# RWKV-7 and pooling layer on one core: the per-pair bonus goes through DRAM, nine gate projections before the dense stage instead of four, and a new order of the work

## The chip, the cores and the metric

The kernel runs on one core of a Trainium2 chip. The metric is the device time of one execution in microseconds (us). The kernel before takes 1591.02 us, the median of three runs (1590.69 to 1591.06).

## The reference

The function computes one inference step of two layers on T = 576 tokens, 512 of a prompt and 8 x 8 of sampled sequences. Each layer is a residual branch behind an RMS norm. The first is RWKV-7 time mixing, in short:

```python
r, k, v, z = xr @ w_r, xk @ w_k, xv @ w_v, xg @ w_z           # 1024 -> 2048 each
decay = exp(-exp(-softplus(-(w0 + tanh(xw @ w1) @ w2)) - 0.5))
a = sigmoid(a0 + (xa @ a1) @ a2)
# per head of 64, over the tokens in turn:
Sa = S @ a_t                                                  # a_t is -kk, b_t is kk * a
S = S * w_t + Sa[:, None] * b_t + v_t[:, None] * k_t ;  y_t = S @ r_t
y = group_norm(y) * gn_g + gn_b
bonus = sum(r * k * r_k, per head) * v
out = ((y + bonus) * silu(z)) @ w_o                           # 2048 -> 1024
```

The second layer is a causal pooling mixer: u, z = x @ w_in, averages of u over windows of 2, 4, 8 and 16 tokens, a grouped product, a SiLU gate and an output product. A last norm and the new states are the other outputs.

## The kernel before, in words

The 2048 inner channels are 16 "pairs" of heads, 128 channels each, on the 128 partitions; KC is 16. A projection of one pair is 8 slices of the input (KD) times two halves of 288 tokens (HT) times three matmuls (high by high, high by low, low by high part of fp32): 48 matmuls. Casts on ScalarE make the high part of the weights (wh), subtractions on VectorE or GpSimd the low part (wl).

The work comes in four stretches.

- **The front**, a loop over the pairs: the k and r projections (L493), low-rank products for decay and a (L576), the scan L of log decays (L622), and from its exponentials Pc, Pp and Pi the scaled operands: RAt (L643 from r, L670 from the normed k), BK (L679), its scaled copy BS and the transposes BT (L694), and rk (L658). RAt, BK, BT and rk are spilled to DRAM by SP.
- **The recurrence**, a loop over the pairs with the tokens in chunks of 64. `vproj(m)` projects v for a pair (L875, `oov`), stores vs and its transpose, loads rk and makes the bonus: a product over the head (L902, `oob`), a product with vs in place (L906) and the addition of gn_b (L910). `prep(m)` makes the chunk matrices (L941, `paA`) and inverts them: a loop on GpSimd (L1012, L1018) on X, X to the DRAM tile xd (L1025), the blocks TI back (L1032), transposes T of them on VectorE (L1039), small products `paz` and `pax`. `recur(m)` runs the chain of eight steps, one per chunk: PE state product L1124, ScalarE rhs L1137, PE TI product L1141, ScalarE UV L1146, PE product with BKT L1157, VectorE state update L1169. The outputs `yy` (L1240, L1245) go beside it. `after(m)` normalises y; its last step is L1336 (`pay`) and L1341, which adds vs, the bonus, and the result is written to yb_d (L1346).
- **The gates**. `zgate(m)` projects z for m below NZ = 4 (L1362, `ooz`), takes the SiLU (L1367) and writes z_d (L1371). The other twelve are projected in the dense stage (`gz`, L343 to L345) with their SiLU at L1438.
- **The dense stage**: yb and, for m below NZ, z are read back, GpSimd multiplies them (L1439), the product is cast (GH); then w_o (`go`), the pooling layer and the norms.

Everything up to the gates is registered as an operation of a plan; `Plan.order` emits them by a heap on a number, WHEN of the operation's label plus STEP times the pair, out of the table OFFS. An operation is emitted only when what it needs has been emitted and a buffer of each kind in its list `use` is free. So the table sets the order of the instructions on every engine, SP's DMA queue among them. The dense stage is ordered by the tile scheduler. There, z uses the five buffers with the tag "t" (`ctmp`, L1401), yb three, and the products of `proj` six PSUM banks, two to a gate.

Of the kernel before, what the change touches and what calls it, by code (L numbers as in the profile page):

```python
# [46 lines left out]
def constants():  # L47
# [26 lines left out]
    for rho in range(3):  # L74
# [9 lines left out]
F_STEP, R_STEP, Z_STEP = 18.2314, 26.0177, 19.4548  # L84
# [17 lines left out]
    ),  # L102
# [7 lines left out]
    ),  # L110
# [7 lines left out]
    ),  # L118
# [15 lines left out]
    ),  # L134
    "x": (
        "44.02 336.91 19.73 "
# [1469 lines left out]
```

## Time and profile before

| what | us |
|---|---|
| median of three runs | 1591.02 |
| lowest and highest | 1590.69, 1591.06 |
| the profiled execution, its own time | 1591.95 |
| its span, first to last instruction | 1590.1 |
| TensorE busy | 1404.9 (88%) |
| VectorE busy | 899.1 (57%) |
| ScalarE busy | 672.5 (42%) |
| GpSimd busy | 623.3 (39%) |

The span is what lies between the first and the last instruction in the trace. A busy share is an average over the whole span, in which the stretches differ: the front lies at about 0 to 404 us, the recurrence at about 479 to 1002, the gates at 1002 to 1101, and the rest of the dense stage ends at 1590. In a row of a timeline the first number is the start, the second the duration in us, then engine, line, operation, the tile written and the tiles read, and how many instructions were merged; in brackets stands the idle time of the engine just before, and what ended it.

### The profile page before, as it was taken

Reading aid. Unit: us, or ns where it says so; the run is one execution under the profiler, and the core shown is the slowest. Engines: PE = TensorE matmul, PEld = TensorE weight load, DVE = VectorE, ACT = ScalarE, POOL = GpSimd, SP = SyncE. Lnnn points to the kernel's source line nnn. Section 1 sums busy time; section 2 is a strip of 40 time slices with the busy share of each in tenths; the row PEclk is TensorE's granted clock in tenths of the full one; section 3 lists DMA queues with packets and bytes.
Section 4 is the critical chain, followed back from the end, with each engine's and each line's share of the span. In section 5 each row is a group of like instructions: output and inputs, shape, how many; then the busy total and the mean of one; then the engine's idle time right before and its main releaser. Section 6 shows DMA issues by size and latency. Waiting matters only on the chain.

```text
span 1590.1 us, 31516 instructions
## 1 busy us (share of the span) xinstructions
PE 1404.9 (88%) x12032; PEld 1276.7 (80%) x12032; DVE 899.1 (57%) x1840; ACT 672.5 (42%) x1683; POOL 623.3 (39%) x1297
## 2 busy tenths in 40 slices
PE   3678989998458888998889888999999999999996
PEld 2568989998447776776677756899999999999995
DVE  5877777677464655666566654353335474555223
ACT  3453655655114555555555553243223423334221
POOL 1025666665217656665666650042001141443000
PEclk8668999999678999999999986999999999999998
DMA  3025655556657667766777664463223232222221
GB/s 131 17 109 188 223 195 186 176 176 233 209 126 166 150 158 167 163 160 164 166 159 172 147 167 135 137 229 101 80 80 94 88 102 84 90 88 96 80 68 72
DMA packets 236751, 219.86 MB, mean 138 GB/s; under 512 B 149772, under 2 KB 184312, under 8 KB 236472
## 3 DMA queue, kind: packets, MB, share of 16 engines
q1 hardware_dynamic: 236600, 217.84, 48.3%
q8 instruction: 95, 1.56, 0.4%
q14 instruction: 56, 0.46, 0.1%
HBM read 151.76 MB, written 66.02 MB: 137 GB/s over the span
## 4 chain that ended last, share of the span: by engine, by line
PE 62%; DVE 16%; ACT 10%; issue 4%; POOL 3%; DMA 3%; SPq 1%; ACTq 0%; DVEq 0%; POOLq 0%
PE oov L875 4%; PE ch L1157 3%; PE ch L1141 3%; PE paA L941 3%; PE ch L1124 3%; DVE RAt L670 3%; PE zz L345 2%; PE u L345 2%; PE go L345 2%; PE go L343 2%; PE oo L345 2%; PE oo L343 2%; PE u L344 2%; PE u L343 2%; PE zz L344 2%
## 5 line engine op out<-in xcount | busy, mean ns | idle before, releaser
L1012 POOL TENSOR_TENSOR tm<-X,R 108x84 f32<-108x84 f32 (+23 forms) x465 | 148.7, 320 | 176.2 <-DMA xd<-X 77.8
L1018 POOL TENSOR_TENSOR X<-X,tm 108x84 f32<-108x84 f32 (+23 forms) x465 | 155.3, 334 | 36.4
L875 PE MATMUL oov<-X,wh_o 128*128 128x288 f32 x512 | 123.7, 330 | 18.9 <-ACT wh_o L773 18.9
L1169 DVE SCALAR_TENSOR_TENSOR SV<-SV,pcs,ch 64x64 f32<-64x64 f32 x192 | 53.8, 280 | 131.5 <-PE ch L1157 128.9
L329 ACT CAST wh_z<-wf_z 128x1024 fp32r<-128x1024 f32 x42 | 44.2, 1052 | 182.9 <-PE go L344 63.6
L493 PE MATMUL kvk<-X,wh_z 128*128 128x288 f32 x480 | 103.4, 309 | 2.1 <-DVE X L475 2.1
L330 DVE TENSOR_TENSOR wl_z<-wf_z,wh_z 128x1024 fp32r<-128x1024 f32 x42 | 60.3, 1435 | 72.7 <-ACT wh_z L329 72.7
L875 PEld LDWEIGHTS oov<-X,wh_o 128*128 128x128 f32 x512 | 83.3, 199 | 21.5 <-ACT wh_o L773 19.3
L1141 PE MATMUL ch<-rhs,TI 128*128 128x128 f32 x256 | 64.7, 336 | 27.6 <-ACT rhs L1137 23.4
L329 ACT CAST wh_o<-wf_o 128x1024 fp32r<-128x1024 f32 x42 | 44.2, 1053 | 103.2 <-issue 30.8
L1157 PEld LDWEIGHTS ch<-UV,BKT 128*128 128x128 f32 x256 | 40.0, 195 | 58.3 <-ACT UV L1146 45.6
L493 PEld LDWEIGHTS kvk<-X,wh_z 128*128 128x128 f32 x480 | 82.5, 202 | 2.3 <-DVE X L475 2.3
L1157 PE MATMUL ch<-UV,BKT 128*128 128x128 f32 x256 | 62.8, 328 | 23.2 <-ACT UV L1146 19.4
L493 PE MATMUL kvr<-X3h,wh_o 128*128 128x256 f32 (+1 forms) x256 | 80.8, 315 | 0.6 <-ACT wh_o L773 0.6
L493 PE MATMUL kvr<-X3h,wl_o 128*128 128x256 f32 (+1 forms) x256 | 78.5, 306 | 2.9 <-DVE wl_o L777 2.5
L1439 POOL TENSOR_TENSOR yb<-yb,z 128x576 f32<-128x576 f32 x16 | 29.7, 1867 | 130.6 <-DMA z<-z_d 95.2
L493 PE MATMUL kvr<-X3l,wh_o 128*128 128x256 f32 (+1 forms) x256 | 78.1, 305 | 0.0
L875 PE MATMUL oov<-X,wl_o 128*128 128x288 f32 x256 | 77.8, 304 | 0.2 <-DVE wl_o L777 0.2
L1141 PEld LDWEIGHTS ch<-rhs,TI 128*128 128x128 f32 x256 | 39.7, 195 | 44.9 <-ACT rhs L1137 40.8
L493 PE MATMUL kvk<-X,wl_z 128*128 128x288 f32 x240 | 73.7, 307 | 0.0
L1146 ACT COPY UV<-ch 64x64 f32<-64x64 f32 x256 | 53.2, 208 | 47.3 <-PE ch L1141 45.1
L941 PE MATMUL paA<-RA,BK 64*128 64x128 f32 x576 | 60.1, 312 | 13.4 <-DVE RA L974 3.8
(319 smaller groups left out, 4738.2 us busy)
## 6 DMA issues: line engine op xcount, KB each, us to landing
bk_d<-BK SPq DMA_DIRECT2D x16, 576.0 KB
ra_d<-RAt SPq DMA_DIRECT2D x16, 576.0 KB
bkt_d<-BT SPq DMA_DIRECT2D x64, 144.0 KB
RA<-ra_d SPq DMA_DIRECT2D x32, 288.0 KB
BK<-bk_d SPq DMA_DIRECT2D x16, 576.0 KB
BKT<-bkt_d SPq DMA_DIRECT2D x64, 144.0 KB
wf_o<-in_w_r SPq DMA_DIRECT2D x16, 512.0 KB
wf_o<-in_w_v SPq DMA_DIRECT2D x16, 512.0 KB
```

What stands on the lines that cost most here:

```text
L329: (hi_eng or S).copy(out=hi, in_=src) if (hi_eng or S) is S else hi_eng.tensor_copy(hi, src)
L330: (lo_eng or V).tensor_tensor(out=lo, in0=src, in1=hi.bitcast(F32), op=ALU.subtract)
L343: PE.matmul(out, wh, xh, start=first, stop=False)
L344: PE.matmul(out, wh, xl, start=False, stop=False)
L345: PE.matmul(out, wl, xh, start=False, stop=last)
L493: PE.matmul(o, w_[:, k, :rows], x_[:, c0:c1], start=k == 0 and i == 0, stop=k == KD - 1 and i == 2)
L875: PE.matmul(buf(*pk)[:, :HT], w_[:, k, :], hs(x_, h), start=k == 0 and i == 0, stop=k == KD - 1 and i == 2)
L941: PE.matmul(pts[q][:, c - c0, :], buf("BK", m)[r0:r0 + 64, c, :], ra(m, q, c), start=True, stop=True)
L1012: E.tensor_tensor(out=tm[:, :nq, :nt], in0=X[:, :nq, s:s + 1].broadcast_to([108, nq, nt]), in1=R[:, s:s + 1, s + 1:].broadcast_to([108, nq ...
L1018: E.tensor_tensor(out=X[:, :nq, s + 1:], in0=X[:, :nq, s + 1:], in1=tm[:, :nq, :nt], op=ALU.add)
L1141: PE.matmul(tile()[:, lo + 128:lo + 256], TI[:, c, :], buf(*rk), start=True, stop=True)
L1157: PE.matmul(buf(*ck)[:, 256:384], buf("BKT", m)[:, c], buf("UV", m)[:, :, c, :], start=True, stop=True)
```

## The change

Three things change. The bonus of a pair (vs after L910) is written by SP to a new DRAM tile bv_d, and `after` reads it back into a tile vr of two buffers, which L1341 uses; vs has two buffers instead of four, and the matmuls of the v projection count as users of vs. NZ is 9 instead of 4. And the whole table OFFS and its steps are new (two lines of it stand for all).

```diff
-F_STEP, R_STEP, Z_STEP = 18.2314, 26.0177, 19.4548
+F_STEP, R_STEP, Z_STEP = 17.1191, 29.6201, 28.3583
...
-        "-16.37 603.57 140.77 382.00 360.77 1129.03 152.36 -54.00 92.74 1132.20 291.83 68.40 1063.08 386.45 151.82 "
+        "-151.11 95.56 101.96 -88.30 -67.95 631.36 -20.94 612.15 -192.57 533.35 634.24 563.57 -145.54 31.51 -124.91 "
...
-NTI, NRA, NW3, NVS, NZ = 3, 4, 4, 4, 4
+NTI, NRA, NW3, NVS, NZ = 3, 4, 4, 2, 9
...
+    bv_d = [dp.tile([128, T], F32, name=f"bv_d{i}") for i in range(KC)]
...
-           "vs": ([128, T], NVS), "vt": ([128, 2, 9, 32], 1), "rk": ([128, T], 1), "zs": ([128, T], 1),
+           "vs": ([128, T], NVS), "vr": ([128, T], 2), "vt": ([128, 2, 9, 32], 1), "rk": ([128, T], 1), "zs": ([128, T], 1),
...
-                mms.append(op("PE", 400, f, need=ws[k // 4] + [xve[k]] + mms[-1:], use=[pk, (f"WO{k // 4}", "v", m)], due=due + .1 * (8 * h + k),
+                mms.append(op("PE", 400, f, need=ws[k // 4] + [xve[k]] + mms[-1:], use=[pk, uvs, (f"WO{k // 4}", "v", m)], due=due + .1 * (8 * h + k),
...
+        def f():
+            SP.dma_start(out=bv_d[m], in_=vs())
+        by["bv", m] = op("SP", 1000, f, need=by["bv", m], use=[uvs], due=due + 7)
...
-        ug, uv = ("sq", m, 1), ("vs", m)
-        lv = by["bv", m]
+        ug, uv = ("sq", m, 1), ("vr", m)
+        n0, plan.n = plan.n, 60
+
+        def f():
+            SP.dma_start(out=buf(*uv), in_=bv_d[m])
+        lv = [op("SP", 1000, f, need=[by["bv", m]], use=[uv], due=due)]
+        plan.n = n0
...
-                                       in1=buf("vs", m)[:, 64 * c0:64 * c1], op0=ALU.mult, op1=ALU.add)
+                                       in1=buf("vr", m)[:, 64 * c0:64 * c1], op0=ALU.mult, op1=ALU.add)
```

Line numbers of the changed kernel are one higher than those of the kernel before up to the bonus, five higher from there, ten higher from the group norm on. Three places show the new order.

**TensorE, the boundary of two pairs in the recurrence.** `ch` is the chain's PSUM tile, one number per pair. Before, from the state product of a pair's last step to the next pair's first:

```order
L1124 MATMUL ch_7299<-SV_6987,RA_5952 128x128
L1048 MATMUL paz_7690<-T_7626,AB_6839 32x32 x16
L1141 MATMUL ch_7299<-rhs_7_7685,TI_4144 128x128
L902 MATMUL oob_1_7713<-rk_7253,cst 128x288
L902 MATMUL oob_0_7717<-rk_7253,cst 128x288
L1157 MATMUL ch_7299<-UV_7015,BKT_7175 128x128
L1062 MATMUL pax_7732<-TI_4145,ZM_7707 32x32 x16
L875 MATMUL oov_1_7750<-X_63,wh_o 128x288 x2
L875 MATMUL oov_1_7750<-X_63,wl_o 128x288
L875 MATMUL oov_1_7750<-X_63,wh_o 128x288 x2
L875 MATMUL oov_1_7750<-X_63,wl_o 128x288
L1124 MATMUL ch_7766<-SV_7454,RA_6419 128x128
```

Now, from the state product of the pair's seventh step on:

```order
L1129 MATMUL ch_7262<-SV_7089,RA_6271 128x128
L1129 MATMUL ch_7732<-SV_7559,RA_6741 128x128
L1146 MATMUL ch_7262<-rhs_6_7730,TI_4165 128x128
L876 MATMUL oov_0_7424<-X_63,wh_o 128x288 x2
L876 MATMUL oov_0_7424<-X_63,wl_o 128x288
L1162 MATMUL ch_7262<-UV_7119,BKT_6949 128x128
L903 MATMUL oob_0_7755<-rk_7675,cst 128x288
L1053 MATMUL paz_7757<-T_7726,AB_6907 32x32 x16
L1129 MATMUL ch_7262<-SV_7089,RA_6271 128x128
L903 MATMUL oob_1_7793<-rk_7675,cst 128x288
L1346 MATMUL pay_1_7796<-cst,yc_7403 64x64 x8
L1146 MATMUL ch_7262<-rhs_7_7788,TI_4165 128x128
```

and, fourteen rows further:

```order
L946 MATMUL paA_4_0_7876<-RA_7681,BK_7683 128x128
L946 MATMUL paA_4_1_7877<-RA_7681,BK_7683 128x128
L946 MATMUL paA_4_0_7876<-RA_7681,BK_7683 128x128
L946 MATMUL paA_4_1_7877<-RA_7681,BK_7683 128x128
L1162 MATMUL ch_7262<-UV_7119,BKT_6949 128x128
L1146 MATMUL ch_7732<-rhs_0_7734,TI_4166 128x128
```

The next pair's first state product (L1129 into ch_7732) stands ahead of the seventh step's TI product, the two `oob` stand behind the products with BKT, and the next pair's first TI product (L1146) directly follows the last product with BKT (L1162).

**VectorE, one pair of the front.** Before, from the scan L on:

```order
L622 SCALAR_TENSOR_TENSOR L_2600<-scan,sg 128x592
L694 STREAM_TRANSPOSE BT_2569<-BS_2538 128x9x2x32
L643 TENSOR_TENSOR RAt_2656<-kvr_0_2602,Pc_2648 64x5x64 x2
L670 SCALAR_TENSOR_TENSOR RAt_2656<-ks_2370,dv,Pp_2662 64x9x64 x2
L643 TENSOR_TENSOR RAt_2656<-kvr_1_2514,Pc_2648 64x4x64 x2
L679 TENSOR_TENSOR BK_2685<-kh_2682,Pi_2624 128x9x64
L658 SCALAR_TENSOR_TENSOR rk_2687<-kvr_1_2514,par,kh_2682 128x256
L658 SCALAR_TENSOR_TENSOR rk_2687<-kvr_0_2602,par,kh_2682 128x320
L592 TENSOR_SCALAR rc_2740<-ss_2733 96x12
```

Now:

```order
L623 SCALAR_TENSOR_TENSOR L_2611<-scan,sg 128x592
L671 SCALAR_TENSOR_TENSOR RAt_2616<-ks_2370,dv,Pp_2613 64x9x64 x2
L695 STREAM_TRANSPOSE BT_2622<-BS_2619 128x9x2x32 x2
L644 TENSOR_TENSOR RAt_2616<-kvr_0_2590,Pc_2665 64x5x64 x2
L644 TENSOR_TENSOR RAt_2616<-kvr_1_2562,Pc_2665 64x4x64 x2
L659 SCALAR_TENSOR_TENSOR rk_2718<-kvr_0_2590,par,kh_2691 128x320
L659 SCALAR_TENSOR_TENSOR rk_2718<-kvr_1_2562,par,kh_2691 128x256
L680 TENSOR_TENSOR BK_2722<-kh_2691,Pi_2652 128x9x64
L612 SCALAR_TENSOR_TENSOR kq_2502<-ks_2370,dv,sn_0_2740 128x288
```

The two L670 operations (now L671) have moved from behind the first products of RAt to directly behind the scan.

**ScalarE, the entry of the dense stage.** Before:

```order
L1438 ACTIVATE z_11918<-gz_0_11922 128x288
L329 CAST wh_z<-wf_z 128x1024
L1438 ACTIVATE z_11918<-gz_1_11947 128x288
L329 CAST wh_o<-wf_o 128x1024
L329 CAST GH<-yb_11888 128x576
L1438 ACTIVATE z_11979<-gz_0_11983 128x288
L1438 ACTIVATE z_11979<-gz_1_12008 128x288
L329 CAST GH<-yb_11895 128x576
L1438 ACTIVATE z_12040<-gz_0_12044 128x288
L329 CAST GH<-yb_11902 128x576
```

Now, from the cast of the first dense weights on:

```order
L329 CAST wh_z<-wf_z 128x1024
L1377 ACTIVATE zs_12203<-ooz_1_12205 128x288
L329 CAST wh_z<-wf_z 128x1024
L329 CAST wh_o<-wf_o 128x1024
L329 CAST GH<-yb_12252 128x576
L329 CAST GH<-yb_12259 128x576
L329 CAST GH<-yb_12266 128x576
L329 CAST wh_z<-wf_z 128x1024
L329 CAST GH<-yb_12273 128x576
L329 CAST GH<-yb_12280 128x576
L1448 ACTIVATE z_12317<-gz_0_12321 128x288
```

The first SiLU of a gate projected in the dense stage (L1448 now, L1438 before) stood ahead of the first cast GH; now it stands behind five of them.

Elsewhere: the v projection of a pair still ends two pairs ahead, and its last matmuls stand in pair 13; `oob` has moved from the pair itself to two pairs ahead. On SP, the reads of vr, of a quarter of BKT and of rk now stand between the writes of xd and the reads of TI. From the first matmul of `go` on no engine's order has changed.

## Rows read from the trace of the kernel before

**Rows 1.** Busy time by stretch: one front pair, one recurrence pair, gates, the rest.

```profile
core 0: us, PE busy (x) PEld busy (x) DVE busy (x) ACT busy (x) POOL busy (x), PEclk, DMA share, GB/s
264.93:283.08 18.15, 17.44 (x133) 16.81 (x133) 12.70 (x18) 10.21 (x23) 11.07 (x13) 1.00 0.54 179
...
706.40:738.80 32.40, 29.09 (x347) 23.10 (x346) 20.40 (x61) 17.62 (x63) 20.86 (x66) 1.00 0.70 162
...
1024.80:1101.30 76.50, 76.47 (x576) 76.47 (x577) 31.00 (x27) 28.71 (x49) 27.51 (x15) 1.00 0.59 195
1101.30:1590.10 488.80, 473.96 (x3522) 470.02 (x3520) 221.47 (x324) 142.65 (x184) 90.36 (x105) 0.99 0.26 84
```

**Rows 2.** Chain of waits by line, within one front pair (283.08 to 301.22).

```profile
by line: DVE RAt L670 33.5%; DVE L L622 9.3%; issue 9.0%; PE kvr L493 8.9%; PE sw L576 7.1%; DVE rk L658 5.2%; ACT kh L648 4.8%; DVE RAt L643 4.7%; ACT kq L552 4.3%; ACT ta L580 4.3%; ACT Pi L629 4.3%; DVE BT L694 4.3%; DVE BK L679 4.2%; AC
```

**Rows 3.** Timeline of TensorE, pairs 7 and 8 of the recurrence.

```profile
760.05 0.49 PE L1124 MATMUL ch<-SV,RA 128*128 128x128 f32 x2
...
761.95 0.49 PE L1157 MATMUL ch<-UV,BKT 128*128 128x128 f32 x2 [0.52 <-ACT UV L1146]
...
763.13 0.49 PE L1124 MATMUL ch<-SV,RA 128*128 128x128 f32 x2
...
767.50 0.49 PE L1141 MATMUL ch<-rhs,TI 128*128 128x128 f32 x2
767.83 1.14 PE L902 MATMUL oob<-rk,cst 128*128 128x288 f32 x4
769.11 0.49 PE L1157 MATMUL ch<-UV,BKT 128*128 128x128 f32 x2
...
771.05 0.38 PE L1124 MATMUL ch<-SV,RA 128*128 128x128 f32 x2
771.36 0.49 PE L941 MATMUL paA<-RA,BK 64*128 64x128 f32 x4
...
774.54 0.49 PE L1141 MATMUL ch<-rhs,TI 128*128 128x128 f32 x2
```

**Rows 4.** Timeline of SP and VectorE in pair 8: xd, TI, L1341, transposes.

```profile
783.73 1.45 SPq L1025 DMA_DIRECT2D xd<-X  x3
788.90 1.80 SPq L1032 DMA_DIRECT2D TI<-xd  x4
...
792.91 0.54 DVE L1341 SCALAR_TENSOR_TENSOR sq<-pay,par,vs 128x320 f32<-128x320 f32 x1
...
795.27 0.91 DVE L1039 STREAM_TRANSPOSE T<-TI 64x256 f32<-64x256 f32 x2
```

**Rows 5.** All L670 operations: shortest, median and longest ns, first and last start.

```profile
L670 DVE SCALAR_TENSOR_TENSOR RAt<-ks,dv,Pp x18: 809/819/2631, 264.9 to 406.3; 64x576 f32<-64x576 f32 x18
```

**Rows 6.** Timeline of GpSimd beside the L670 operations of one pair.

```profile
283.13 0.73 POOL L565 TENSOR_TENSOR ll<-lf,lh 96x256 fp32r<-96x256 f32 x1
283.82 1.28 POOL L777 TENSOR_TENSOR wl_o<-wf_o,wh_o 128x512 fp32r<-128x512 f32 x1
```

**Rows 7.** Timeline of TensorE, ScalarE and GpSimd from the gates into the dense stage.

```profile
1009.40 0.40 PE L1362 MATMUL ooz<-X,wl_z 128*128 128x288 f32 x1 [0.26 <-DVE wl_z L777]
...
1024.83 0.40 PE L343 MATMUL gz<-X,wh_z 128*128 128x288 f32 x1 [1.32 <-ACT zs L1367]
...
1031.65 0.41 ACT L1438 ACTIVATE z<-gz 128x288 f32<-128x288 f32 x1 [6.87 <-PE gz L345]
...
1041.41 0.68 ACT L329 CAST GH<-yb 128x576 fp32r<-128x576 f32 x1 [2.63 <-POOL yb L1439]
...
1039.95 4.71 POOL L1439 TENSOR_TENSOR yb<-yb,z 128x576 f32<-128x576 f32 x3 [95.24 <-DMA z<-z_d]
1046.75 5.45 POOL L1439 TENSOR_TENSOR yb<-yb,z 128x576 f32<-128x576 f32 x3 [2.08 <-DMA yb<-yb_d]
```

**Rows 8.** Timeline of SP and VectorE at the first pair's TI.

```profile
469.76 1.80 SPq L1032 DMA_DIRECT2D TI<-xd  x4
...
473.26 0.91 DVE L1039 STREAM_TRANSPOSE T<-TI 64x256 f32<-64x256 f32 x2 [6.37 <-DMA TI<-xd]
```

More of the change, by code (lines that the diff above doesn't have):

```diff
@@ L87 @@
     "s": (
[14 rows of a table removed]
[13 rows of a table added]
     ),
     "g0": (
[6 rows of a table removed]
[6 rows of a table added]
     ),
     "g1": (
[6 rows of a table removed]
[6 rows of a table added]
     ),
     "f": (
[6 rows of a table removed]
[6 rows of a table added]
     ),
     "e": (
[6 rows of a table removed]
[6 rows of a table added]
     ),
     "x": (
-        "44.02 336.91 19.73 "
+        "125.02 116.05 49.68 "
     ),
     "p": (
[8 rows of a table removed]
[8 rows of a table added]
     ),
     "v": (
-        "523.57 1040.30 854.62 1041.49 129.97 1050.03 1050.15 1052.16 1054.58 -11.47 1063.70 1064.27 1066.70 429.73 "
-        "1043.85 1031.21 1049.44 1053.03 1055.05 1059.61 1058.09 1065.52 166.08 1044.70 70.84 74.27 374.57 419.80 "
-        "1042.69 1121.40 429.26 1139.32 1120.68 66.40 1026.65 "
+        "490.19 531.12 527.84 532.83 -112.45 538.37 538.11 543.05 547.18 -47.55 555.18 556.90 560.36 561.56 535.91 "
+        "-89.79 538.53 544.24 546.14 554.86 -36.96 556.90 21.20 556.90 -74.53 -187.33 138.86 -181.42 555.22 561.25 "
+        "-230.65 562.80 562.47 -77.48 565.04 -318.29 "
     ),
     "c": (
[8 rows of a table removed]
[8 rows of a table added]
     ),
     "o": (
-        "-16.37 603.57 140.77 382.00 360.77 1129.03 152.36 -54.00 92.74 1132.20 291.83 68.40 1063.08 386.45 151.82 "
-        "-153.18 1134.73 98.25 89.73 185.29 1110.79 1134.06 994.42 1144.50 1072.56 1155.82 "
[3 rows of a table added]
     ),
     "y": (
-        "1496.73 1503.45 67.64 1505.39 58.47 1505.69 1086.16 1509.62 "
+        "1034.50 1043.91 0.32 1022.28 116.00 1029.10 482.43 1057.96 "
     ),
     "z": (
-        "1450.95 67.43 197.50 90.55 1484.35 1127.54 171.35 975.59 155.00 1473.82 1496.06 409.58 450.91 190.92 1498.08 "
-        "1002.12 1504.12 87.17 133.84 436.59 406.24 1111.84 1108.83 1019.99 "
+        "1018.95 1021.87 1030.19 1037.69 1036.94 1041.83 1042.12 -42.15 1042.68 1047.39 533.11 1048.28 1047.67 "
+        "-218.40 1049.68 1048.36 1048.24 1050.32 -144.58 1051.39 -61.30 1049.12 1060.25 57.96 "
     ),
```

109 rows, old and new, of the table OFFS are left out of this document.

## The prediction, made before the change was run

> **What bounds the kernel now.** I read the busy time by stretch first [rows 1]. From 1101.30 us on TensorE is busy 473.96 of 488.80 us; on every engine the instruction order of that stretch, from the first w_o product on, is unchanged, so I cost it at nothing. In the gate stretch before it (1024.80 to 1101.30) TensorE is busy 76.47 of 76.50 us: this part is bounded by matmuls and nothing else. Ahead of that lie two loops over the 16 pairs. One pair of the front takes 18.15 us [rows 1], with TensorE busy 17.44 of it; its chain of waits gives VectorE's two L670 operations 33.5% [rows 2]. One pair of the recurrence takes 32.40 us. There TensorE is busy 29.09 us, VectorE 20.40, ScalarE 17.62, GpSimd 20.86 and the DMA engines 70% [rows 1]: none is full, so the eight-step chain and what TensorE does in its gaps set the time. A bare step is the distance from one state product L1124 at 760.05 to the next at 763.13 [rows 3], 3.08 us; in it TensorE idles 0.52 us for ScalarE's UV, and from L1157 to the next L1124 it has 1.18 us to fill.
>
> The profiled execution took 1591.95 us, 0.93 above the median of the three runs, 1591.02; 1.85 us of it lie outside the span of 1590.1. The sum is made on 1591.95, and 0.93 comes off at the end. A difference under 0.2%, 3.2 us, is about what a measurement of this kernel cannot tell from no change.
>
> **The spill and the read-back.** Sixteen writes and sixteen reads of 128x576 f32 (0.295 MB each) are added, 0.59 MB a pair. In the recurrence DMA moves 162 GB/s over 32.4 us [rows 1], 5.25 MB a pair, so this is 11% more; 70% busy becomes about 78%. I cost the traffic at nothing: the idle 30% hides it. Without that cover it would be 0.59 MB at 162 GB/s, 3.6 us a pair. No compute instruction is added by it, and the final L1341 only waits for a DMA where it waited for ScalarE. VectorE holds, behind L1341, the state update L1169: a late read would stop the chain; this is a rival below. The read goes out after the xd writes, which end being issued at 785.18 in pair 8, and L1341 comes at 792.91 [rows 4], 7.7 us later.
>
> **Does v run further ahead?** By the order it does not: the v projection stays two pairs ahead, with the same number of matmuls in nearly every gap, and still ends in pair 13; only the bonus product oob moves, from the pair itself to two pairs ahead. So pairs 14 and 15 stay poorly filled, as now; I cost them at 0, with 3 us either way.
>
> **The pair boundary.** Here the new order bites. Now, from the last TI product of a pair (767.50) to the first of the next (774.54) TensorE takes 7.04 us [rows 3] and has hardly a gap in it: two oob, L1157, pax, six oov, L1124, four paA, 32 yy, sixteen paA. In the new order the next pair's L1124 is issued one step earlier, and both oob go between L1157 and the following TI product of the last two steps. The oob take the 1.28 us from 767.83 to 769.11 and L1124 the 0.31 from 771.05 to 771.36 [rows 3]; 7.04 - 1.28 - 0.31 = 5.45 us are left between the two TI products. That saves 1.6 us a pair if the two oob and the extra L1124 fill gaps that are empty now, and nothing if they push the chain by their own length. They do some of both: an oob of 0.64 us fits into the 1.18 us from L1157 to L1124, but the other stands between L1124 and the TI product beside eight pay, and the step that takes in the second L1124 keeps three oov as well. Between 0 and -1.6 I take -0.7, for 14 pairs -10 us; ends -22 and, with the delay of the slower rival, +11.
>
> **The front.** The two L670 move from behind ScalarE's kh to just behind the scan L, so they leave the place where the chain has them; the rest (kh on GpSimd, rk, BK, kq, ta, rc on VectorE, rb and td on ScalarE, then L) stays. TensorE has 17.44 us of work in 18.15 [rows 1], so at most 0.71 us a pair is to be had before TensorE binds. I take half, -0.35, for 14 pairs -5 us. Ends: -10 (all of it), and +7 (0.5 a pair: a second long L670 costs 1.8 us, 2.63 less 0.82 [rows 5], and VectorE's idle 5.45 of 18.15 us, estimated, takes up the other seven tenths).
>
> L670 takes 0.819 us in the median and 2.631 at the longest; the long one of a pair lies beside two GpSimd operations, 0.73 and 1.28 us from 283.13 on [rows 6]. The Trainium skill, page "SBUF — State Buffer", section "Who interferes with whom", has it that a VectorE instruction with two SBUF inputs and a GpSimd one that reads SBUF exclude each other for the whole instruction. The trace agrees in kind: L670 is lengthened by 1.8 us, about the 2.0 us of the two GpSimd operations. By that rule the move frees nothing where GpSimd reads SBUF beside the new place too; the front's term would be 0 in place of -5 and the time 1590 us.
>
> **The gates.** Nine gates are now projected ahead instead of four, but the order puts only 57 of their matmuls ahead of the last L1157, where 63 stood before; the rest stand behind it. TensorE does them either way. The stretch from the last step to w_o now holds 129 + 576 = 705 gate matmuls, and 375 + 336 = 711 after: +6 at 76.50/576 = 0.133, +0.8 us. For each early gate ScalarE now has the Silu of its second half ahead of the cast that the next gate needs, where the casts stood ahead before; a wait for wl_z showed as 0.26 us [rows 7], so for seven gates I take +1.2.
>
> Then the dense entry. The nine spilled gates come back through the five buffers "t"; ScalarE's order has the casts GH of the first five products yb*z ahead of gate 9's Silu. GpSimd's first product starts 15.1 us after the first gz matmul (1039.95 against 1024.83), its fourth at 1046.75, each then 5.45/3 = 1.82 us [rows 7]. So the fifth ends at 1046.75 + 3.6 = 1050.4, 25.5 after the first gz matmul; with a cast of 0.68 and a Silu of 0.41 gate 9's bank comes free at 26.6. Three gates fill the six PSUM banks: 3 x 48 x 0.133 = 19.1 us. TensorE waits 7.5 us at gate 12, where it does not wait anywhere now. It ends cheapest at +2, if the reads come sooner, and dearest at +14, if the third buffer of yb delays the fourth product as well. Gates together: 0.8 + 1.2 + 7.5 = +9.5, taken as +9, since six matmuls leave pair 15.
>
> **Sum.** -10 - 5 + 9 = -6 on 1591.95 gives 1585.9; less 0.93, **1585.0 us**.
>
> **Rivals.**
> 1. *Both loops reach TensorE's floor*: -22 and -10 with +9, -23: 1568 us. For it: TensorE idles 3.3 us a pair of the recurrence. Against it: seven of eight steps keep their waits.
> 2. *Lock*: L670 beside GpSimd stays three times as long as without it (2.63 against 0.82 us), as GpSimd is busy 11.07 of a front pair's 18.15 us [rows 1], so L670 meets it in the new place as well and pushes the loop there. The front gains nothing: -10 + 9 = -1, 1590 us. Against it: GpSimd has its weight subtractions in another place now.
> 3. *Slower: TI comes late.* SP now issues the read of the bonus, a BKT part and the read of rk (0.72 MB) between the xd writes and TI's reads. Now TI is issued from 788.90 to 790.70 and VectorE transposes it at 795.27, 4.6 us later [rows 4]; in the first pair, where it waits for this DMA, the transposes followed the last issue by 1.7 us (471.56 to 473.26 [rows 8]), so 2.9 us are spare. At 162 GB/s the 0.72 MB take 4.4 us. If they delay TI by more than 2.9, by the full 4.4, VectorE stops 1.5 us a pair with L1169 behind the transposes: +21 - 10 = +11 for the recurrence, and +11 - 5 + 9 = +15: 1606 us. Against it: SP waits 3.7 us for xd (785.18 to 788.90) in which most of the 0.72 MB can go. The Trainium skill, page "DMA: Bandwidth & Descriptors", section "Queues, rings and completion order", says that each DMA engine consumes descriptors in ring order; no row here shows one transfer behind another; by it TI would queue behind the reads, and the time would be these 1606 us.
> 4. *The change does what it says*, five gates hidden in the recurrence: -5 x 48 x 0.133 = -32 in place of +9: -47, 1544 us. The order speaks against it.
>
> **Chances.** Forecast 0.45, floor 0.14, lock 0.18, TI late 0.20, hidden gates 0.03. The forecast's own range is 1575 to 1595; about two thirds of it lie below 1587.8, a fifth within 0.2%. With the floor and the hidden gates whole, and the lock's case mostly within 0.2%, faster has 0.51, same 0.19, slower 0.30. The range 1567 to 1603 leaves out the hidden gates, half of the floor's case and half of the late TI's.
>
> **What would show it.** Right: a pair of the recurrence near 31.5 us with the distance between the boundary's TI products near 5.5; a front pair near 17.8; TensorE waiting some 7 us for ScalarE at gate 12. Wrong: VectorE waiting for TI or for the bonus read (rival 3); L670 still 2.6 us and on the front's chain (lock); the boundary at 7 us, which would leave only the gates' loss, 1591.0 - 5 + 9 = 1595 us.

## The result, and the profile after

The changed kernel takes 1563.08 us, the median of four runs (1559.35 to 1564.77); the kernel before took 1590.86 in the runs beside it (1587.66 to 1591.06). The ratio is 0.983, with a 95% interval of 0.981 to 0.985: 28 us faster, where 6 were forecast. It lies under the stated range. The profiled execution took 1564.77 us, its span is 1562.9.

Where the time went is read from the starts of a few instructions in both traces: the first and the last scan L of the front, the first and the last product with BKT of the recurrence (L1157, now L1162), and the first matmul of w_o.

| stretch, us | before | after | difference |
|---|---|---|---|
| start to first scan | 113.2 | 113.6 | +0.4 |
| first to last scan (front) | 288.0 | 266.5 | -21.5 |
| last scan to first product with BKT | 84.8 | 89.2 | +4.4 |
| first to last product with BKT (recurrence) | 515.8 | 493.3 | -22.5 |
| last product with BKT to w_o (gates) | 99.6 | 111.4 | +11.8 |
| w_o to the end | 488.7 | 488.9 | +0.2 |

The table of busy times after has one row each for a front pair, a pair of the recurrence, the early gates, the gates of the dense stage, and the rest; the columns are those of [rows 1]:

```profile
331.70:348.40 16.70, 16.70 (x134) 16.70 (x133) 11.29 (x19) 9.90 (x22) 12.46 (x14) 1.00 0.58 193
684.80:715.50 30.70, 28.88 (x345) 22.76 (x345) 20.29 (x61) 17.23 (x63) 20.56 (x65) 1.00 0.77 190
962.90:1017.05 54.15, 52.43 (x413) 51.01 (x411) 15.54 (x36) 16.00 (x32) 0.00 (x0) 1.00 0.35 118
1017.05:1073.95 56.90, 47.36 (x336) 46.89 (x337) 26.55 (x22) 20.07 (x34) 24.53 (x15) 0.91 0.68 240
1073.95:1562.90 488.95, 473.97 (x3522) 470.02 (x3520) 221.54 (x325) 142.40 (x184) 90.30 (x105) 0.99 0.26 84
```

This front pair takes 16.70 us where one took 18.15 (the steady ones now take 16.4 to 16.7, but for one of 18.3 with more matmuls in it), a pair of the recurrence 30.7 where it took 32.4 (30.79 against 32.33 as the median distance between pairs). In this front pair TensorE is busy without a gap (over the whole front 257.6 of 266.5 us), and the chain of waits, which gave L670 33.5% [rows 2], has only matmuls:

```profile
by line: PE kvr L494 39.1%; PE kvk L494 38.7%; PE sn L606 7.9%; PE ss L588 5.6%; PE sw L577 4.8%; PE sa L577 4.8%
```

At the boundary of two pairs TensorE's timeline now has the next pair's first state product at 734.43 (each of these matmuls leaves two records; the four of L1129 are the step's own product and this one) and the two `oob` at 736.66 and 738.19, all ahead of the last TI product at 739.38; in [rows 3] they came behind it:

```profile
734.43 0.71 PE L1129 MATMUL ch<-SV,RA 128*128 128x128 f32 x4
735.33 0.49 PE L1146 MATMUL ch<-rhs,TI 128*128 128x128 f32 x2 [0.19 <-ACT rhs L1142]
...
736.33 0.49 PE L1162 MATMUL ch<-UV,BKT 128*128 128x128 f32 x2
736.66 0.65 PE L903 MATMUL oob<-rk,cst 128*128 128x288 f32 x2
737.24 0.69 PE L1053 MATMUL paz<-T,AB 32*32 32x32 f32 x32
737.86 0.49 PE L1129 MATMUL ch<-SV,RA 128*128 128x128 f32 x2
738.19 0.65 PE L903 MATMUL oob<-rk,cst 128*128 128x288 f32 x2
738.77 0.69 PE L1346 MATMUL pay<-cst,yc 128*64 128x64 f32 x16
739.38 0.49 PE L1146 MATMUL ch<-rhs,TI 128*128 128x128 f32 x2
739.80 0.69 PE L1067 MATMUL pax<-TI,ZM 32*32 32x32 f32 x32
...
744.92 0.39 PE L1146 MATMUL ch<-rhs,TI 128*128 128x128 f32 x2
```

From the last TI product at 739.38 to the next pair's first at 744.92 it takes 5.54 us, where it took 7.04 [rows 3]; the step before it, TI product to TI product, takes 739.38 - 735.33 = 4.05, where it took 3.47. TI does not come late, as SP and VectorE show (to be read beside [rows 4]):

```profile
755.31 1.33 SPq L1030 DMA_DIRECT2D xd<-X  x3
756.68 0.58 SPq L1334 DMA_DIRECT2D vr<-bv_d  x1
757.31 0.43 SPq L1109 DMA_DIRECT2D BKT<-bkt_d  x1
757.79 1.28 SPq L896 DMA_DIRECT2D rk<-rk_d  x1
760.02 1.82 SPq L1037 DMA_DIRECT2D TI<-xd  x4
...
763.67 0.54 DVE L1351 SCALAR_TENSOR_TENSOR sq<-pay,par,vr 128x320 f32<-128x320 f32 x1
...
765.24 0.90 DVE L1044 STREAM_TRANSPOSE T<-TI 64x256 f32<-64x256 f32 x2
```

SP issues the reads of vr, BKT and rk while it waits for xd, TI goes out 3.38 us after the last xd write was issued (760.02 against 756.64; before 3.7), and the transposes follow 3.4 us behind its last issue without a wait. Over the whole recurrence VectorE waited for this transfer once, 0.5 us.

In the gates TensorE waits as foreseen, a little longer, once for the SiLU of gate 9; the wait for zs was there before, 1.32 us [rows 7]. The columns are who waited, for what, us in total, times, longest:

```profile
PE gz L343 <- ACT z L1448: 9.2, 1, 9.2
PE gz L343 <- ACT zs L1377: 1.3, 1, 1.3
```

GpSimd's fourth product starts late, for yb's fourth transfer, and the SiLU stands behind the cast GH of the fifth on ScalarE (to be read beside [rows 7]):

```profile
1032.31 4.69 POOL L1449 TENSOR_TENSOR yb<-yb,z 128x576 f32<-128x576 f32 x3 [124.30 <-DMA z<-z_d]
1041.76 4.63 POOL L1449 TENSOR_TENSOR yb<-yb,z 128x576 f32<-128x576 f32 x3 [4.77 <-DMA yb<-yb_d]
...
1044.55 0.67 ACT L329 CAST GH<-yb 128x576 fp32r<-128x576 f32 x1 [0.68 <-POOL yb L1449]
1045.12 0.70 ACT L1448 ACTIVATE z<-gz 128x288 f32<-128x288 f32 x2
```

After the wait TensorE has the lower clock for a time, as the busy times before, in and after it show (the first gz matmul is at 1017.1, 144 matmuls later the wait begins):

```profile
1017.10:1036.40 19.30, 19.30 (x144) 19.08 (x144) 5.14 (x5) 3.44 (x4) 4.09 (x3) 1.00 0.84 318
1036.40:1045.60 9.20, 0.04 (x2) 0.02 (x1) 4.78 (x5) 3.44 (x6) 4.43 (x4) 0.72 0.89 335
1045.60:1052.00 6.40, 6.40 (x31) 6.40 (x32) 3.87 (x3) 3.39 (x8) 4.26 (x4) 0.61 0.48 140
```

At the granted 0.61, 31 matmuls take 6.40 us, where 144 took 19.30 before: 0.206 us each against 0.134, or 2.2 us for the 31. Wait and clock are 9.2 + 2.2 = 11.4 of the 11.8 us by which the stretch is longer.

### The profile page after: what moved, and what is told of

It reads as the page before. It is cut to its first block, busy times and chain, and to the rows that moved or that the text cites. A ratio compares the mean times of both kernels' runs of the same rounds, so it can differ in the third digit from the quotient of the medians.

```text
span 1562.9 us, 31586 instructions
## 1 busy us (share of the span) xinstructions
PE 1399.9 (90%) x12032; PEld 1275.2 (82%) x12032; DVE 889.8 (57%) x1845; ACT 664.8 (43%) x1688; POOL 628.1 (40%) x1297
## 4 chain that ended last, share of the span: by engine, by line
PE 65%; DVE 17%; ACT 9%; DMA 4%; issue 3%; POOL 1%; SPq 1%; DVEq 0%; ACTq 0%; POOLq 0%
PE kvk L494 5%; PE kvr L494 4%; PE ooz L1372 3%; PE ch L1146 3%; PE oov L876 3%; PE zz L345 2%; PE go L343 2%; PE u L345 2%; PE oo L345 2%; PE go L345 2%; PE u L344 2%; PE zz L344 2%; PE oo L343 2%; PE u L343 2%; PE oo L344 2%
## 5 line engine op out<-in xcount | busy, mean ns | idle before, releaser
L1017 POOL TENSOR_TENSOR tm<-X,R 108x84 f32<-108x84 f32 (+23 forms) x465 | 153.6, 330 | 155.9 <-DMA R<-rd 99.6
L494 PE MATMUL kvk<-X,wh_z 128*128 128x288 f32 x480 | 104.7, 308 | 22.5 <-ACT X L472 20.4
L329 ACT CAST wh_o<-wf_o 128x1024 fp32r<-128x1024 f32 x39 | 41.0, 1050 | 175.2 <-PE go L344 63.7
L330 DVE TENSOR_TENSOR wl_o<-wf_o,wh_o 128x1024 fp32r<-128x1024 f32 x39 | 57.8, 1481 | 51.9 <-ACT wh_o L329 51.9
L494 PE MATMUL kvr<-X3h,wh_o 128*128 128x320 f32 (+1 forms) x256 | 79.6, 311 | 1.9 <-ACT wh_o L774 1.4
L494 PE MATMUL kvr<-X3h,wl_o 128*128 128x320 f32 (+1 forms) x256 | 79.1, 309 | 0.9 <-DVE wl_o L778 0.9
L1162 PEld LDWEIGHTS ch<-UV,BKT 128*128 128x128 f32 x256 | 40.5, 197 | 47.3 <-ACT UV L1151 35.4
L494 PE MATMUL kvr<-X3l,wh_o 128*128 128x320 f32 (+1 forms) x256 | 78.8, 308 | 0.0
L1162 PE MATMUL ch<-UV,BKT 128*128 128x128 f32 x256 | 63.6, 332 | 16.3 <-ACT UV L1151 11.3
L1146 PE MATMUL ch<-rhs,TI 128*128 128x128 f32 x256 | 63.7, 332 | 11.9 <-ACT rhs L1142 10.7
L1129 PE MATMUL ch<-SV,RA 128*128 128x128 f32 x256 | 61.0, 331 | 12.3 <-DVE SV L1174 6.5
L330 DVE TENSOR_TENSOR wl_z<-wf_z,wh_z 128x1024 fp32r<-128x1024 f32 x40 | 51.8, 1295 | 32.5 <-ACT wh_z L329 32.4
## 6 DMA issues: line engine op xcount, KB each, us to landing
RA<-ra_d SPq DMA_DIRECT2D x32, 288.0 KB
```

Source lines behind the costliest of these rows:

```text
L329: (hi_eng or S).copy(out=hi, in_=src) if (hi_eng or S) is S else hi_eng.tensor_copy(hi, src)
L330: (lo_eng or V).tensor_tensor(out=lo, in0=src, in1=hi.bitcast(F32), op=ALU.subtract)
L494: PE.matmul(o, w_[:, k, :rows], x_[:, c0:c1], start=k == 0 and i == 0, stop=k == KD - 1 and i == 2)
L1017: E.tensor_tensor(out=tm[:, :nq, :nt], in0=X[:, :nq, s:s + 1].broadcast_to([108, nq, nt]), in1=R[:, s:s + 1, s + 1:].broadcast_to([108, nq ...
L1129: PE.matmul(tile()[:, lo:lo + 128], buf("RA", m)[:, c, 64:192], buf("SV", m)[:, :, c, :], start=True, stop=True)
L1146: PE.matmul(tile()[:, lo + 128:lo + 256], TI[:, c, :], buf(*rk), start=True, stop=True)
```

## The experiments

All twelve runs are in one table. The ratio is to the kernel before, run beside them. The kernel before itself had medians of 1587.86 to 1590.86 us in these sessions, so where two rows differ by 3 us or less the stretches and the ratios say more than the totals. In the diffs a number such as c.69 or f.76 is one entry of the table OFFS, by its group and place. Front, pair and gates are read from each trace as above (front: first to last scan; pair: median distance of the recurrence's pairs; gates: last product with BKT to w_o).

| kernel | us | ratio (95%) | front | pair | gates |
|---|---|---|---|---|---|
| before | 1590.86 | 1 | 288.0 | 32.33 | 99.6 |
| the change | 1563.08 | 0.983 (0.981 to 0.985) | 266.5 | 30.79 | 111.4 |
| e1_front | 1570.74 | 0.987 (0.985 to 0.990) | 266.6 | 32.26 | 99.6 |
| e2_rest | 1582.97 | 0.995 (0.993 to 0.997) | 286.5 | 30.80 | 111.1 |
| e3_nz4 | 1549.35 | 0.974 (0.971 to 0.976) | 266.1 | 30.80 | 97.7 |
| e4_nospill | 1565.32 | 0.984 (0.981 to 0.986) | 266.5 | 30.80 | 112.3 |
| e5_boundary | 1577.32 | 0.994 (0.992 to 0.996) | 266.7 | 31.43 | 116.5 |
| e6_l671 | 1592.48 | 1.001 (1.000 to 1.003) | 294.1 | 30.80 | 110.0 |
| e7_rhslater | 1567.45 | 0.987 (0.985 to 0.988) | 266.2 | 31.04 | 110.0 |
| e8_t8 | 1555.55 | 0.980 (0.977 to 0.982) | 266.3 | 30.80 | 99.6 |
| e9_simple | 1549.80 | 0.976 (0.974 to 0.978) | 267.5 | 30.80 | 97.7 |
| e10_z30 | 1565.69 | 0.986 (0.984 to 0.988) | 266.3 | 30.80 | 93.0 |
| e11_z45 | 1593.07 | 1.003 (1.002 to 1.005) | 266.7 | 30.79 | 94.0 |
| e12_l670 | 1577.02 | 0.991 (0.988 to 0.995) | 269.6 | 32.32 | 99.6 |

**The two loops apart.** e1_front puts the new groups s, g0, g1, f, e, x and F_STEP into the kernel before; e2_rest puts the old ones into the changed kernel.

> The kernel before with the changed kernel's order of the front alone (the groups s, g0, g1, f, e and x of the table and F_STEP); no spill, four early gates, the old order from the v projection on. Theory: the three pieces of the change are independent, and the front gives 16 to 21 us by itself: front pairs of 16.7 us, recurrence pairs still 32.3, total about 1573 us (1568 to 1577). Rival: the front is faster only because the new order of the recurrence takes loads and casts out of it; then front pairs stay near 18.1 and the total is within 3 us of 1591.

> The changed kernel with the old order of the front. Theory: recurrence pairs of 30.8 us (-22 in all) and a gate stretch that is 12 us longer, so about 1580 us (1576 to 1585), with front pairs back at 18.1. Rival: the recurrence is faster only behind the new front (its spills land earlier); then its pairs are back near 32.3 and the total is about 1600.

Both theories hold: the front alone gives 1570.74 us, the rest alone 1582.97, and each leaves the other loop as it was (pairs of 32.26 us, a front of 286.5). The two gains over 1590.4, the kernel before in those runs, are 19.7 and 7.5 us; together 27.2, and the change gives 27.8. The pieces add up. The 4.4 us between the last scan and the recurrence belong to the rest: that stretch takes 91.9 us in e2_rest and 85.9 in e1_front (84.8 before, 89.2 in the change). What makes it longer was not tried.

**The early gates.** e3_nz4:

```diff
-NTI, NRA, NW3, NVS, NZ = 3, 4, 4, 2, 9
+NTI, NRA, NW3, NVS, NZ = 3, 4, 4, 2, 4
```

> The changed kernel with NZ = 4: five gates go back to the dense stage. Theory: the nine early gates cost 12 us, most of it one wait of 9.2 us of TensorE for the SiLU of gate 9; with four of them the stretch from the last step to w_o is 99 us again and the total about 1552 us (1549 to 1556). Rival: the early gates pay, because their matmuls fill the last pairs; then this is slower than the changed kernel, 1565 to 1575.

1549.35 us: the five gates cost 13.7 us where they are now, as the total and the stretch of the gates (111.4 against 97.7) both have it. The busy times of the whole stretch from the last product with BKT to w_o show TensorE with 1.3 us idle:

```profile
959.60:1057.30 97.70, 96.38 (x752) 95.82 (x751) 39.47 (x52) 34.90 (x61) 28.20 (x15) 1.00 0.54 176
```

e8_t8 keeps nine early gates and takes the wait away by its cause:

```diff
-    def ctmp(nm, w=T, tag="t", bufs=5):
+    def ctmp(nm, w=T, tag="t", bufs=8):
```

> The changed kernel, nine early gates, with eight buffers of tag t in place of five in the dense stage. Theory: the wait of 9.2 us at gate 12 comes from gate 9's SiLU, which has to wait for the fifth product yb*z to free a buffer; with eight it waits for the second, TensorE no longer stops, and the total falls by 8 to 10 us, to about 1554. Rival: the wait is the transfers' (z and yb landing late); then it stays, within 3 us of 1563.

The wait is gone and the stretch is as short as before, 99.6 us: so the wait came from the buffers. The median falls by 7.5 us to 1555.55, near the 8 to 10 foreseen, and the stretch alone by 11.8. In the profiled execution, which at 1561.24 us was the slowest of the four (the others took 1553.33 to 1555.91), w_o and what follows take 494.5 us where the change took 488.9. TensorE's waits there, of the gates and then of w_o:

```profile
PE gz L343 <- ACT zs L1377: 1.3, 1, 1.3
...
PE go L344 <- DVE GL L330: 1.9, 2, 1.0
```

The first 15 us of w_o, in e8_t8 and then in the change:

```profile
1064.90:1080.00 15.10, 13.02 (x78) 12.34 (x76) 9.13 (x9) 6.54 (x10) 8.89 (x5) 0.80 0.43 121
```

```profile
1073.95:1089.00 15.05, 15.05 (x115) 15.05 (x114) 5.91 (x8) 5.26 (x7) 2.16 (x1) 1.00 0.24 79
```

GpSimd multiplies there still (8.89 us of 15.10 against 2.16), w_o waits for the low parts GL of the products, the clock falls to 0.80, and 78 matmuls are done where 115 were: 37 x 0.133 = 4.9 of the 5.6 us. In this execution, with the matmuls gone from the dense stage, the products bound its start. Whether the three faster ones lost as much there is not known, as they left no trace.

**The spill.** e4_nospill keeps vs in four buffers:

```diff
-NTI, NRA, NW3, NVS, NZ = 3, 4, 4, 2, 9
+NTI, NRA, NW3, NVS, NZ = 3, 4, 4, 4, 9
...
-        ug, uv = ("sq", m, 1), ("vr", m)
+        ug, uv = ("sq", m, 1), ("vs", m)
+        lv = by["bv", m]
```

> The changed kernel with vs kept in four buffers and L1341 reading it there: no write of the bonus to DRAM and no read back. The order on TensorE, VectorE, ScalarE and GpSimd is the same. Theory: the spill neither costs nor gives anything, within 3 us of the changed kernel (1560 to 1566), pairs of 30.8 us. Rival 1: its 9.4 MB of transfers cost something, 3 to 10 us faster without. Rival 2: the spill is what carries the gain of the recurrence; then pairs go back toward 32.3 us and the total to 1575 to 1585.

1565.32 us and pairs of 30.80: the spill neither gains nor costs anything that these runs tell. e9_simple joins it to NZ = 4, so that only the table is new.

> The changed kernel with NZ = 4 and without the spill: of the change only the new table is left. Theory: spill and early gates add nothing to the gain, so this is as fast as the changed kernel with NZ = 4 alone, 1549 us (1546 to 1553). Rival: the spill matters where the gates do not hide it; then 3 us or more apart from it.

1549.80 us, 0.45 from e3_nz4 (ratios 0.976 and 0.974, whose intervals overlap). Two of the three parts that give the change its name, the spill and the early gates, bring nothing that these runs tell, or cost; its gain is the order.

**The pair boundary.** e5_boundary moves four operations of the table back: the next pair's first state product (c.8), the last product with BKT (c.69) and the two `oob` (v.29, v.32). e7_rhslater moves only the first of them, to another place:

```diff
-c.8  588.97   c.69 626.21   v.29 561.25   v.32 562.47
+c.8  596.04   c.69 622.46   v.29 563.07   v.32 563.12
...
-c.8  588.97
+c.8  594.97
```

> The changed kernel with the old order at the pair boundary: the next pair's first state product behind the six oov of the boundary, both oob and the last product with BKT directly behind the last TI product. Theory: the boundary gives 0.9 us a pair net (7.04 to 5.54 us there, 3.47 to 4.05 us in the step before), the other 0.6 us come from the first three steps and stay; so pairs of 31.7 us and a total of about 1575 us (1572 to 1578). Rival: the saving is not the boundary's; then pairs stay at 30.8 and the total within 3 us of 1563.

> The changed kernel with the next pair's first state product moved from the seventh step to behind the last TI product and pax, ahead of oov and paA. Theory: in the seventh step it costs 0.58 us (4.05 against 3.47), behind the last TI product, where TensorE has work without a gap, only its own 0.3 to 0.4; so pairs of about 30.6 us and 2 to 3 us less in all, 1560 us. Rival: issued later it delays the first TI product of the next pair through ScalarE's copy; then pairs are longer by up to 0.5 us, total up to 1570.

TensorE's TI products at the boundary in e5_boundary, with the two `oob` behind the last of the pair:

```profile
743.03 0.49 PE L1146 MATMUL ch<-rhs,TI 128*128 128x128 f32 x2 [0.41 <-ACT rhs L1142]
...
746.28 0.49 PE L1146 MATMUL ch<-rhs,TI 128*128 128x128 f32 x2
746.60 1.14 PE L903 MATMUL oob<-rk,cst 128*128 128x288 f32 x4
...
752.91 0.49 PE L1146 MATMUL ch<-rhs,TI 128*128 128x128 f32 x2
```

e5_boundary gives pairs of 31.43 us, 0.64 longer and not 0.9: at the boundary 6.63 us (5.54 in the change), in the step before 3.25 (4.05), in the next pair's first step 4.87 (4.58). The boundary is a cause, of at least 0.64 of the 1.54 us a pair; its total, 1577.32, has 5 us from the gates' stretch (116.5 against 111.4) and 3 from the one ahead of the recurrence in it as well. e7_rhslater is a miss: pairs of 31.04 us, longer by 0.25, and the step before the boundary stays at 4.06 us. So the state product costs nothing in that step, where I had put its 0.58 us, and its new place gives 0.2 at the boundary (5.76 against 5.54). In e5_boundary, where both `oob` are behind the last TI product again, that step takes 3.25. The last product with BKT comes behind that step in both, so the 0.8 us belong to the `oob`. How much they give at the boundary was not tried apart from that product.

**L670.** e6_l671 puts the two operations of a steady front pair behind the products with r again; e12_l670 does the opposite in the kernel before (there the line is L670), by putting the exponential Pp first on ScalarE, on which L670 follows at once. One number each, of e6_l671 and then of e12_l670:

```diff
-f.76 102.87
+f.76 124.88
...
-f.67 120.16
+f.67 60.16
```

> The changed kernel with the two L671 operations of a steady front pair moved back behind the products L644 with r and ahead of rk, as they stood before; all else of the front as in the change. Theory: this place is what took them off the loop over L, and the front pair goes back from 16.7 to 18.1 us or more, total 1583 us (1578 to 1600). Rival: the new order of the k and r matmuls on TensorE is what closed its gaps; then the front pair stays within 0.3 us of 16.7 and the total within 5 us of 1563.

> The kernel before with one number of its table changed: the exponential Pp of a steady front pair (f.67) 60 us earlier, so that it comes first behind the scan on ScalarE and the two L670 operations directly behind it on VectorE; all else as before. Theory: L670's place is enough; front pairs of 16.6 to 17.2 us and a total 13 to 20 us under the kernel before, 1569 to 1576 us. Rival: the changed order of the k and r matmuls is needed as well; then front pairs stay above 17.7 and the gain is under 6 us.

e6_l671 loses 29 us, more than the whole front had gained: 18.83 us a pair, with the exponential Pp still first on ScalarE. So it is L671's place on VectorE that counts. VectorE and GpSimd in one pair of it:

```profile
359.60 3.96 DVE L671 SCALAR_TENSOR_TENSOR RAt<-ks,dv,Pp 64x576 f32<-64x576 f32 x1
358.40 1.27 POOL L778 TENSOR_TENSOR wl_o<-wf_o,wh_o 128x512 fp32r<-128x512 f32 x1 [0.40 <-ACT wh_o L774]
359.64 0.73 POOL L566 TENSOR_TENSOR ll<-lf,lh 96x256 fp32r<-96x256 f32 x1
360.32 1.40 POOL L653 TENSOR_TENSOR kh<-ks,kh 128x576 f32<-128x576 f32 x1
361.68 1.27 POOL L778 TENSOR_TENSOR wl_o<-wf_o,wh_o 128x512 fp32r<-128x512 f32 x1
```

VectorE's first L671 takes 3.96 us; the shortest takes 0.81. It begins while GpSimd still works on the first of four operations in a row (358.40 + 1.27 = 359.67) and ends 0.61 us after the last of them (363.56 against 361.68 + 1.27 = 362.95), while GpSimd's take no longer than elsewhere. So it was held by the operation that was running and by three that began after it had. The long ones before, of 2.63 us, lie the same way: GpSimd's kh was still running when they began (for 0.09 us in the pair of [rows 6]), ahead of the two operations in [rows 6], and they end 0.61 us after the second of these. All of these operations, before and in the change ([rows 5] has only those from 264.9 us on):

```profile
L670 DVE SCALAR_TENSOR_TENSOR RAt<-ks,dv,Pp x32: 809/1512/2631, 116.6 to 406.3; 64x576 f32<-64x576 f32 x32
```

```profile
L671 DVE SCALAR_TENSOR_TENSOR RAt<-ks,dv,Pp x32: 809/889/2233, 115.8 to 383.2; 64x576 f32<-64x576 f32 x32
```

e12_l670 is the other half: in the kernel before one number takes the front from 288.0 to 269.6 us, 16.57 to 16.59 us in each of the last steady pairs, and TensorE has no gap left (two pairs of it by busy times, then the chain of waits in one):

```profile
318.70:351.80 33.10, 33.10 (x264) 33.10 (x263) 25.39 (x37) 20.00 (x44) 23.49 (x25) 1.00 0.61 196
```

```profile
by line: PE kvr L493 39.1%; PE kvk L493 38.3%; PE sn L605 7.9%; PE ss L587 5.7%; PE sw L576 4.8%; PE sa L576 4.8%
```

The place of L670 is enough; the order of k and r on TensorE is not needed for it. Whether it is the shorter L670 or its earlier end that counts, these runs don't separate: in steady pairs the two take 2.6 us together and end 3.5 us after the scan in e12_l670, 2.4 and 3.3 in the change, 3.4 and 8.8 before, 4.8 and 9.8 in e6_l671. The median, 1577.02, shows 13 us of the 18. In the profiled execution, the slowest of the four at 1581.07, the recurrence took 5.5 us longer, 5.1 of them in its last two pairs (below), and the stretch ahead of the first scan 1.7.

**Gates into the last pairs.** TensorE has gaps in pairs 14 and 15; e10_z30 and e11_z45 take the late entries of the groups y and z 30 and 45 us forward, with NZ = 4.

> The changed kernel with NZ = 4 and the gates' operations (groups y and z) 30 us earlier in the table: 108 gate matmuls stand ahead of the last L1162 instead of 57. Theory: pairs 14 and 15 have empty gaps on TensorE, at half the clock in part of them (0.50 from 900 to 930 us), so gates put there are nearly free and their 51 matmuls (51 x 0.133 = 6.8 us) leave the stretch behind: 4 to 9 us faster than with NZ = 4 alone, 1541 to 1545 us. Rival: they wait there for their input slices, which land until 930 us, and hold the chain: the same or slower than 1549.

> The same with 45 us: 144 gate matmuls ahead of the last L1162. Theory: 87 matmuls more than in the change (11.6 us), 7 to 13 us faster than with NZ = 4 alone, 1537 to 1542 us. Rival: the first of them stand where their slices have not landed; TensorE then waits inside the chain of pair 14 and the total is 1549 or more.

Both theories fall. The recurrence takes 513.0 and 538.1 us against 491.3 with NZ = 4 alone. TensorE's waits in e10_z30 begin with

```profile
PE ooz L1372 <- DMA X<-xg_d: 11.3, 2, 7.5
```

and the busy times at that place are

```profile
900.00:910.00 10.00, 2.26 (x8) 1.99 (x9) 2.05 (x7) 0.00 (x0) 7.91 (x29) 0.50 1.02 327
910.00:920.00 10.00, 10.00 (x78) 9.71 (x77) 2.92 (x13) 2.48 (x11) 0.06 (x1) 0.65 0.84 202
```

While a gate matmul waits for its slice of the input, the chain behind it stands still: TensorE is busy 2.26 of these 10.00 us. The DMA engines are full (1.02) meanwhile, and TensorE has the lower clock in the wait and behind it (0.50 and 0.65 in these rows). In this order the gates can't start sooner unless their input does. e11_z45 shows the same, with 17.9 us in three waits. The waits are 11.3 of the 21.7 us and 17.9 of the 46.8 us that the recurrence lost; the rest was not taken apart.

The best of these is e3_nz4, 1549.35 us, 41 us under the kernel before.

## Why the prediction was wrong

- **The front: the step that failed.** "TensorE has 17.44 us of work in 18.15 [rows 1], so at most 0.71 us a pair is to be had before TensorE binds." A busy time was taken for work. The same matmuls take 16.70 us now and 16.57 in e12_l670; in 17.44 matmuls that stretch over a wait are counted. Over the whole front it is the same: 1925 records are busy for 265.3 us before, 1921 for 257.6 now. The row had a nearer figure in its next column: the weight loads, 16.81 us [rows 1]. The Trainium skill, page "Perfetto Trace Analysis", section "Identifying the Most-Contended Engine", says that matmul busy time is no good measure of how near TensorE is to its limit, and names the busy share of the weight loads as one of two to use instead. Here the loads come within 0.1 to 0.25 us of what the pair then took, but from above, so they are no floor either. I put -5 us, with an end of -10; it measured -21.5 between the scans and -19.7 as a part alone (e1_front). The sum also took 14 pairs alike: 12.7 of the 21.5 us come in the last nine distances between scans and 8.8 in the first six, among which one of 23.06 us now takes 16.86.
- The mechanism, L670 leaving the chain, was right: e12_l670 shows it to be enough, and e6_l671 takes the gain away. The rival "lock" had its fact right and its conclusion wrong: L670 is long beside GpSimd (e6_l671: 3.96 us), but its new place meets less of GpSimd. The Trainium skill, page "SBUF — State Buffer", section "Who interferes with whom", says that a VectorE instruction with two SBUF inputs and a GpSimd one that reads SBUF exclude each other; I weighed that against the change. The lengths fit it: the old place cost 1.8 us a pair, and the new one 0.8 (0.89 + 1.53 against 2 x 0.81 in most steady pairs).
- **The recurrence: a term mis-sized.** The boundary was forecast at 5.45 us and measured 5.54, so the -1.6 were right, and the step before it lost 0.58, so the net is -0.92 where -0.7 was taken. But the other steps were taken as unchanged, and the first three gave 0.27, 0.20 and 0.14 us more. Together 1.54 a pair, -22.5 in the whole recurrence. That is the end of -22 that I had given, but by another sum, so the agreement is in part luck. 4.4 us go back ahead of the first pair, a stretch for which the sum had no term. The first step's 0.27 belong to the boundary, as e5_boundary takes them back (4.87); what shortened the second and the third step was not tried.
- **The gates** were forecast at +9 and measured +11.8, by the mechanism named. The first product started 15.2 us after the first gz matmul (1032.31 less 1017.1), as taken, but the fourth 24.7 after it, where 21.9 were taken: yb's fourth transfer came later, the end of the term that I had named as its dearest. The SiLU at 1045.12 frees the bank 28.4 us after the first gz matmul and not 26.6, which makes the wait 9.2 for 7.5. What the sum left out is the clock behind the wait, 2.2 us; of the 2.0 us put down for six matmuls and the casts 0.4 are left.
- **The traffic** was hidden, as costed, and the late TI did not happen. The Trainium skill, page "DMA: Bandwidth & Descriptors", section "Queues, rings and completion order", has descriptors consumed in ring order; the three reads did stand ahead of TI, and still VectorE waited for it once in the whole recurrence, 0.5 us. SP had issued them while it waited for xd, so no run here shows that rule at work or against it. The reads are 720 KB, 0.74 MB and not 0.72, which makes the rival's 4.4 us 4.6.
- **The range** ended at 1567, since the floor rival, 1568, took the front's end from the busy time too. With 16.8 for it that rival would have been -22 - 19 + 9 = -32: 1559 us, and a range down to there would have held 1563.

## What to carry to other kernels

A matmul's busy time can hold waits, as in the front here (17.44 us for what then took 16.57 to 16.70). Bound what TensorE can still gain by the loads of weights in the same row as well (16.81), or by the distance of the starts where nothing waits. Where VectorE and GpSimd both read SBUF, look at what GpSimd does beside each place that a VectorE operation could have: one number of an order was worth 18 us of front. Work put early into an engine's order pays only when its inputs have landed and its buffers are free; here five gates more cost 14 us behind five buffers, and four gates put earlier into the chain 16 and 44 us.

## What was not expected of the hardware

The last two pairs of the recurrence take different times without a change of their order. From the first product with BKT of pair 14 to that of pair 15 three kernels with the same order there took 34.4 us (e1_front), 35.7 (before) and 39.4 (e12_l670); over all kernels it was between 32.9 and 39.4 (e10_z30 and e11_z45 aside, which put more gates into it). The busy times of that stretch, of the kernel before and of e12_l670:

```profile
934.90:970.60 35.70, 28.49 (x261) 20.96 (x261) 15.12 (x47) 14.13 (x54) 7.88 (x27) 0.67 0.54 135
```

```profile
918.80:958.30 39.50, 32.57 (x261) 23.35 (x261) 15.07 (x47) 14.09 (x54) 8.36 (x28) 0.53 0.48 119
```

The granted clock is 0.67 in the one and 0.53 in the other (the levels are 1.2 and 2.4 GHz), and 0.70 in e1_front; it was 1.00 in the two pairs before, in which TensorE still had the v projection in its gaps. After that the gaps are empty (TensorE busy 28.49 of 35.70 us, at the lower clock for a part of it). In the change, the same stretch was granted 0.54. What sets which kernel has more of the lower clock there stays open, as each left one trace. The difference is of the size of the spread between runs of one kernel (1559.35 to 1564.77 for the change), so a difference of a few us between two of these totals says little, and the pairs' own distances are the better witness.
